# The product with V as split fp32r products over 128 stationary columns, in a two-layer hybrid attention block

## The chip, the core and the metric

The kernel runs on one core of a Trainium2 chip. The metric is the device time of one execution in microseconds; the time before is the median of three runs. A core has TensorE (PE in the profile; PEld is its weight load), VectorE (DVE), ScalarE (ACT), GpSimd (POOL) and SyncE (SP), which here issues the DMAs. The engines run side by side, each its own instructions in order.

## The reference

Two layers over 1024 latent tokens and 256 context tokens of width 1024. Each layer mixes tokens with three head groups and then applies an MLP. What matters here is the softmax and its product with V, once for each group:

```python
# A: 4 heads, 2 KV heads, windowed (|i-j| <= 128) plus all context keys, with a sink logit
p = softmax(concat([s_loc, s_ctx, sink_logit]))
out = einsum(p[..., :n_loc], vb) + einsum(p[..., n_loc:n_loc + n_ctx], v_ctx)
# B: 4 heads, 2 KV heads, all 1280 keys, RMS-normalised q and k
p = softmax(einsum(qg, k) * dh ** -0.5);  out = einsum(p, v)
# C: 8 heads, low-rank q and kv, shared rotary key of 32
s = einsum(q_nope, k_nope) + einsum(q_rope, k_rope)
p = softmax(s * 96 ** -0.5);              out = einsum(p, v)
```

Head size of V is 64 everywhere. Context queries (layer 0 only) see the context keys alone. The output projection, the residuals, the normalisations and the squared-ReLU MLP of width 4096 are outside the change. All is fp32.

## The kernel before

Tokens are cut into 10 tiles of 128: tiles 0 and 1 are context, 2 to 9 latent. Large products are made of fp32r products of high and low parts: a value x is split into a high part of type fp32r (a copy) and the low part x - high (a subtraction), and three products (high-high, high-low, low-high) stand for one.

A layer runs in stages. The input projection (`Proj`) makes queries, keys and V of A and B for each token tile, and the 416 columns that C starts from, all kept in SBUF. Then comes attention: A and B heads alternately, then the eight C heads, each in windows of one head and its query groups (two groups of four latent tiles; in layer 0 also the group of the two context tiles). The output projection and the MLP follow.

One step of attention (`step`) is one head and one query tile: PE writes the scores of up to 1280 keys into PSUM, DVE takes the maximum (L798, L1012), ScalarE the exponential with the sum (L771), DVE the sum of two partial sums where there are two (C heads, L783) and the reciprocal (L784), and the row is scaled by it. `NORM` says which engine scales: GpSimd for A (L789), DVE for B and C (L791).

The product with V (`Attn.products`, L819) goes over the key tiles of a unit, that is one head and one query group. For each key tile PE transposes the four tiles of P into one of two PSUM banks (`tr`, L827); ScalarE copies the bank to SBUF (`ptS`, L832, three places), which frees the bank; PE multiplies (L842). The product is in fp32: the stationary operand is V, 64 columns, the moving one 256 query columns, and the two halves of the queries go to the two halves of the array's columns (`tile_position`), 2 x 2 matmul records in the profile. The sums of a unit grow in one PSUM bank (`pvb`); DVE copies it to SBUF (`ys`, L866), and two DMAs bring it to memory.

C's preparation (`AttnC`) transposes the low-rank columns, and makes V of all eight heads (`prep_v`, L1230) ahead of the first C head; for each head it makes keys (`prep_k`) and queries (`prep_q`). Where a split has room it leaves its PSUM bank first: ScalarE copies to SBUF, DVE casts the high part (L710 for keys, L1304 for queries), GpSimd subtracts (L713, L1307). The queries' rotary part is turned by DVE and GpSimd (L1293, L1297, L1301).

The order of all this is not written by hand. Each operation is given to `Plan` with its engine, a rough time, what it needs and a key; `Plan.run` plays the operations through on a model of the engines and emits them in the order of their starts. At run time each engine keeps to that order. GpSimd cannot pass an instruction that waits, nor can DVE or ScalarE.

## Time and profile before

| | us |
|---|---|
| median of three runs | 3544.21 (3541.7 to 3546.61) |
| span of the profiled execution | 3540.4 |
| the span's busy time: PE / DVE / ACT / POOL | 3398.3 / 2011.7 / 1290.8 / 856.1 |
| scores of A and B: first start to last end, layer 0; layer 1 | 228.9 to 463.9; 2120.0 to 2328.9 |
| last product with V, layer 0; layer 1 | 869.0; 2715.4 |

The median lies 3.8 us above the profiled span. A row that groups instructions gives line, engine, operation, output and inputs by the program's names, partitions x elements, count; behind the bar busy time and the mean of one in ns, then the engine's idle time ahead of them and what ended it. The busy time of matmuls counts overlapping ones once; their own ends are modelled, so rows of the timeline are read from start to start.

### The profile page before, as it was taken

Reading aid. Unit: us, or ns where it says so; the run is one execution under the profiler, and the core shown is the slowest. Engines: PE = TensorE matmul, PEld = TensorE weight load, DVE = VectorE, ACT = ScalarE, POOL = GpSimd, SP = SyncE. Lnnn points to the kernel's source line nnn. Section 1 sums busy time; section 2 is a strip of 40 time slices with the busy share of each in tenths; the row PEclk is TensorE's granted clock in tenths of the full one; section 3 lists DMA queues with packets and bytes.
Section 4 is the critical chain, followed back from the end, with each engine's and each line's share of the span. In section 5 each row is a group of like instructions: output and inputs, shape, how many; then the busy total and the mean of one; then the engine's idle time right before and its main releaser. Section 6 shows DMA issues by size and latency. Waiting matters only on the chain. (4 is left out here: it accounts for less than half of the span.)

```text
span 3540.4 us, 46962 instructions
## 1 busy us (share of the span) xinstructions
PE 3398.3 (96%) x18628; PEld 2577.9 (73%) x18628; DVE 2011.7 (57%) x3640; ACT 1290.8 (36%) x2568; POOL 856.1 (24%) x690
## 2 busy tenths in 40 slices
PE   7999999999899999999997999999998899999998
PEld 4776666665778787888885886666665778888887
DVE  3466777775763333333437656766676854444446
ACT  2136666665322121212121226666665222222222
POOL 1243332220421010111015433332223611111113
PEclk9999999999999999999998999999999999999999
DMA  7500100004213332201113200000014011111121
GB/s 259 161 8 11 29 8 8 9 28 129 85 66 102 96 95 90 90 30 48 36 36 126 90 1 8 28 8 7 7 50 141 24 42 48 48 48 48 51 87 48
DMA packets 155677, 206.99 MB, mean 58 GB/s; under 512 B 9808, under 2 KB 107584, under 8 KB 154432
## 3 DMA queue, kind: packets, MB, share of 16 engines
q1 hardware_dynamic: 152576, 192.12, 17.1%
q10 hardware_dynamic: 2736, 11.80, 0.8%
q8 instruction: 146, 2.39, 0.3%
q14 instruction: 75, 0.61, 0.1%
q0 software_dynamic: 144, 0.07, 0.0%
HBM read 179.86 MB, written 24.15 MB: 58 GB/s over the span
## 5 line engine op out<-in xcount | busy, mean ns | idle before, releaser
L1794 DVE TENSOR_TENSOR acc<-acc,o 128x512 f32<-128x512 f32 x518 | 332.6, 683 | 406.6 <-PE o L1783 406.5
L106 POOL TENSOR_TENSOR al<-r,ah 128x512 fp32r<-128x512 f32 x136 | 159.8, 1175 | 1184.0 <-ACT ah L105 1099.4
L832 ACT COPY ptS<-tr 128x512 f32<-128x512 f32 (+2 forms) x624 | 336.5, 552 | 273.9 <-PE tr L827 268.9
L1783 PE MATMUL o<-w2h,ah 128*128 128x512 f32 x1080 | 342.9, 398 | 11.0 <-ACT ah L105 7.7
L1783 PE MATMUL o<-w2h,al 128*128 128x512 f32 x1080 | 334.9, 391 | 0.7 <-DVE al L106 0.6
L1783 PE MATMUL o<-w2l,ah 128*128 128x512 f32 x1080 | 335.4, 392 | 0.0
L1675 DVE TENSOR_TENSOR r<-r 128x512 f32<-128x512 f32 x150 | 102.4, 682 | 368.3 <-ACT r L1674 368.3
L1661 PE MATMUL tr<-hTl,w1h 128*128 128x512 f32 (+1 forms) x856 | 307.3, 359 | 4.4 <-DVE hTl L1579 4.4
L827 PE MATMUL tr<-ident,PB 128*128 128x128 f32 x1920 | 303.6, 283 | 4.9 <-DVE PB L791 3.7
L1661 PE MATMUL tr<-hTh,w1h 128*128 128x512 f32 (+1 forms) x856 | 307.1, 359 | 0.0
L1661 PE MATMUL tr<-hTh,w1l 128*128 128x512 f32 (+1 forms) x856 | 306.8, 358 | 0.0
L827 PEld LDWEIGHTS tr<-ident,PB 128*128 128x128 f32 x1920 | 211.4, 141 | 130.9 <-issue 109.0
L1327 PE MATMUL c<-kb,cq 96*128 96x512 f32 (+1 forms) x1200 | 288.3, 371 | 4.3 <-ACT PC L771 2.5
L798 DVE TENSOR_REDUCE nx<-c 128x1 f32<-128x256 f32 (+1 forms) x272 | 214.2, 793 | 103.4 <-PE c L1327 96.2
L105 ACT CAST w2h<-w2s 128x1024 fp32r<-128x1024 f32 x58 | 60.9, 1050 | 539.6 <-DVE w2s L1653 332.3
L1327 PEld LDWEIGHTS c<-kb,cq 96*128 96x128 f32 x1200 | 196.9, 188 | 76.1 <-issue 18.4
L1783 PEld LDWEIGHTS o<-w2h,ah 128*128 128x128 f32 x1080 | 197.9, 189 | 60.1 <-ACT ah L105 8.8
L1783 PEld LDWEIGHTS o<-w2h,al 128*128 128x128 f32 x1080 | 203.2, 188 | 46.0 <-DVE al L106 2.1
L1783 PEld LDWEIGHTS o<-w2l,ah 128*128 128x128 f32 x1080 | 203.6, 189 | 44.3
L842 PE MATMUL pvb<-ptS,vc 128*64 128x256 f32 x1344 | 215.5, 401 | 10.8 <-ACT ptS L832 8.9
L771 ACT ACTIVATE PB<-c,nx 128x256 f32<-128x256 f32 (+1 forms) x256 | 202.4, 798 | 28.2 <-DVE nx L748 27.4
L1503 PE MATMUL o<-wo,hTh 128*128 128x512 f32 x576 | 184.1, 401 | 0.0
(485 smaller groups left out, 6602.9 us busy)
## 6 DMA issues: line engine op xcount, KB each, us to landing
mw<-in_w_mod SPq DMA_DIRECT2D x80, 512.0 KB
w1s<-in_w_fc SPq DMA_DIRECT2D x62, 512.0 KB
w2s<-in_w_fc SPq DMA_DIRECT2D x62, 512.0 KB
yf<-ydr SPq DMA_DIRECT2D x18, 512.0 KB
wst<-in_w_in SPq DMA_DIRECT2D x16, 512.0 KB
ydr<-ys SPq DMA_DIRECT2D x128, 64.0 KB
wos<-in_w_out SPq DMA_DIRECT2D x16, 512.0 KB
x1dr<-xt SPq DMA_DIRECT2D x10, 512.0 KB
```

Source lines behind the costliest of these rows:

```text
L106: (el or V.tensor_tensor)(out=lo, in0=src, in1=f32(hi), op=OP.subtract)
L771: S.activation(out=st["P"][:, o:o + w], in_=f(), func=AF.Exp, scale=scale, bias=st["nx"][:, 0:1], accum_out=st["sm"][:, i:i + 1])
L798: V.tensor_reduce(out=st["nx"][:, i:i + 1], in_=view, axis=AX.X, op=OP.max, negate=True)
L827: PE.transpose(ptp[:, j * 128:(j + 1) * 128], u["P"][j][:, pc(j):pc(j) + 128], ident)
L832: S.copy(out=st["t"][:, c0:c1], in_=ptp[:, c0:c1])
L842: PE.matmul(pvb[64 * half:64 * half + 64, c0 - b:c1 - b], lhsT=u["V"](tt), rhs=st["t"][:, c0:c1], start=(idx == 0), stop=(idx == len(kts) ...
L1327: PE.matmul(p, lhsT=a[:, qs], rhs=b[:, c0:c1], start=(n == 0), stop=(n == 2), skip_group_check=True)
L1503: PE.matmul(p, lhsT=self.place(t, a, k // 4)[:, k % 4, :], rhs=self.wo[n, k][b], start=(k == 0 and first), stop=(k == 7 and last))
L1661: PE.matmul(p[:, 0:w], lhsT=a[:, k, :], rhs=o.hT[i][b, k // 4][:, k % 4, :], start=(k == 0 and first), stop=(k == 7 and last))
L1675: V.tensor_tensor(out=r[:, 0:w], in0=r[:, 0:w], in1=r[:, 0:w], op=OP.mult)
L1783: PE.matmul(p[i], lhsT=a[:, ts_], rhs=b[:, i * 512:(i + 1) * 512], start=(first and n == 0), stop=(last and n == 2))
L1794: V.tensor_tensor(out=o, in0=o, in1=p[i], op=OP.add)
```

## The change

The product with V becomes one of split parts. V is stored as 128 stationary columns, 64 of its high part and beside them 64 of its low part, both fp32r. P is split when it leaves the transposes' bank: ScalarE copies the high part as before, now cast to fp32r, and DVE subtracts to get the low part, after which the bank is free. PE multiplies the 128 columns with the high and then with the low part of P, 512 query columns each, in the whole array. Rows 0 to 63 of the bank `pvb` then hold the part from V's high columns, rows 64 to 127 that from the low ones: ScalarE copies the lower rows out, DVE adds the upper ones, and one DMA stores the result.

```diff
-    PTS = 3
+    PTS = 2
-    NORM = {k: [dict(p='POOL', d='DVE')[x] for x in v] for k, v in zip('ABC', 'pppp dddd dddd'.split())}
+    NORM = {k: [dict(p='POOL', d='DVE')[x] for x in v] for k, v in zip('ABC', 'pppp pppp pppp'.split())}
...
             def copied(ptp, st, js):
-                st["t"] = M([128, 512], F32, "ptS", bufs=PTS)
-                S.copy(out=st["t"][:, c0:c1], in_=ptp[:, c0:c1])
+                both = M([128, 2, 512], F32R, "ptS", bufs=PTS)
+                st["t"] = both[:, 0, cols(js)], both[:, 1, cols(js)]
+                S.copy(out=st["t"][0], in_=ptp[:, cols(js)])
+
+            def rest(ptp, st, js):
+                V.tensor_tensor(out=st["t"][1], in0=ptp[:, cols(js)], in1=f32(st["t"][0]), op=OP.subtract)
 
             def product(st, idx):
-                for half in range(2):
-                    PE.matmul(pvb[64 * half:64 * half + 64, c0 - b:c1 - b], lhsT=u["V"](tt), rhs=st["t"][:, c0:c1],
-                              start=(idx == 0), stop=(idx == len(kts) - 1), tile_position=(0, 64 * half),
-                              skip_group_check=True)
+                for n, part in enumerate(st["t"]):
+                    PE.matmul(pvb[:, cols(js)], lhsT=u["V"](tt), rhs=part, start=(idx == n == 0),
+                              stop=(n == 1 and idx == len(kts) - 1), skip_group_check=True)
...
-                cp = plan.add("ACT", t_act(128 * len(js)), lambda tr=tr, st=st, js=js: copied(tr.slot, st, js), [tr], k + KCOPY, "pt", [tr])
+                hi = plan.add("ACT", t_act(128 * len(js)), lambda tr=tr, st=st, js=js: copied(tr.slot, st, js), [tr], k + KCOPY, "pt")
+                lo = plan.add("DVE", t_dve(128 * len(js)), lambda tr=tr, st=st, js=js: rest(tr.slot, st, js), [hi], k + KCOPY, None, [tr])
...
-                V.tensor_copy(st["y"][:, 0:w], pvb[:, 0:w])
+                S.copy(out=st["y"], in_=pvb[64:128, 0:w])
+                V.tensor_tensor(out=st["y"], in0=pvb[0:64, 0:w], in1=st["y"], op=OP.add)
```

All softmax scaling now is GpSimd's: the 192 rows of 1280 and 24 of 256 that DVE scaled join the 72 that GpSimd had. V takes twice the room, so other things are cut smaller or leave SBUF: C's 416 columns go to memory after the projection (`cdr`) and come back in pieces ahead of C (`load_kv`, `load_cq`, eleven loads in all); V of C is made for four heads at a time (`prep_v(half, i)`), the second four while heads 3 and 4 run; the weights of C's queries come in two halves; B's and C's keys lie in tiles of up to 512 tokens, and the projected rows of A and B in two tiles of 512 columns. In the input projection V of A and B is split for each token tile by four small copies on ScalarE and four subtractions on DVE. The finished sums have one place instead of two.

PE's order in the layer 1 C sweep, in a run of rounds without scores between (`tr` are the two banks, `PB` the rows of P, `vc` C's V). Before:

```order
L842 MATMUL pvb<-ptS_15277,vc_451_17077 64x256 x2
L827 MATMUL tr_64<-ident_66,PB_416_15402 128x128
L827 MATMUL tr_64<-ident_66,PB_418_15442 128x128
L827 MATMUL tr_64<-ident_66,PB_419_15494 128x128
L827 MATMUL tr_64<-ident_66,PB_421_15544 128x128
L842 MATMUL pvb<-ptS_15291,vc_452_17117 64x256 x2
```

And now:

```order
L881 MATMUL pvb<-ptS_15950,vc_496_17870 128x512 x2
L865 MATMUL tr_63<-ident_66,PB_420_15861 128x128
L865 MATMUL tr_63<-ident_66,PB_428_15901 128x128
L865 MATMUL tr_63<-ident_66,PB_434_15932 128x128
L865 MATMUL tr_63<-ident_66,PB_442_15989 128x128
L881 MATMUL pvb<-ptS_15959,vc_496_17870 128x512 x2
```

The alternation stays; the two narrow products of a key tile became two wide ones.

DVE's order in the same sweep, from a cast of keys (`kb`) on (`nx` are maxima, `sm` sums, `c` scores). Before:

```order
L710 CAST kb_439_16664<-sp_409_15353 64x512
L798 TENSOR_REDUCE nx_15251<-c_449_0_16989 128x1
L783 TENSOR_TENSOR sm_15239<-sm_15239 128x1
L784 RECIPROCAL sm_15239<-sm_15239 128x1
L798 TENSOR_REDUCE nx_15251<-c_449_1_16990 128x1
L791 TENSOR_SCALAR PB_392_15236<-PB_392_15236,sm_15239 128x1280
L748 TENSOR_SCALAR nx_15251<-nx_15251 128x1
L710 CAST kb_439_16664<-sp_423_15760 64x512
```

And now:

```order
L748 CAST kb_479_17476<-sp_449_16061 64x512
L909 TENSOR_TENSOR ys_16049<-pvb,ys_16049 64x512
L876 TENSOR_TENSOR ptS_15959<-tr_63,ptS_15959 128x512
L837 TENSOR_REDUCE nx_15918<-c_492_0_17794 128x1
L822 TENSOR_TENSOR sm_15904<-sm_15904 128x1
L823 RECIPROCAL sm_15904<-sm_15904 128x1
L837 TENSOR_REDUCE nx_15918<-c_492_1_17795 128x1
L876 TENSOR_TENSOR ptS_15950<-tr_64,ptS_15950 128x512
L787 TENSOR_SCALAR nx_15918<-nx_15918 128x1
L748 CAST kb_482_17579<-sp_457_16471 64x512
```

The scaling (L791) is gone from the piece, and the subtractions (L876) and the addition of finished sums (L909) stand in it.

GpSimd's order there. Before, only the work on keys and queries:

```order
L713 TENSOR_TENSOR kb_439_16664<-sp_409_15353,kb_439_16664 64x512
L713 TENSOR_TENSOR kb_439_16664<-sp_423_15760,kb_439_16664 64x512
L1297 TENSOR_TENSOR qf_16856<-qf_16856,trig_16244 32x512
L1307 TENSOR_TENSOR cq_16841<-qf_16856,cq_16841 96x512
L713 TENSOR_TENSOR kb_439_16664<-sp_389_15229,kb_439_16664 64x256
```

And now:

```order
L828 TENSOR_TENSOR PB_420_15861<-PB_420_15861,sm_15988 128x1280
L751 TENSOR_TENSOR kb_488_17697<-sp_449_16061,kb_488_17697 64x512
L828 TENSOR_TENSOR PB_428_15901<-PB_428_15901,sm_16005 128x1280
L751 TENSOR_TENSOR kb_489_17708<-sp_457_16471,kb_489_17708 64x512
L828 TENSOR_TENSOR PB_434_15932<-PB_434_15932,sm_16043 128x1280
L1359 TENSOR_TENSOR qf_17667<-qf_17667,trig_16978 32x512
L828 TENSOR_TENSOR PB_442_15989<-PB_442_15989,sm_16065 128x1280
L1369 TENSOR_TENSOR cq_17654<-qf_17667,cq_17654 96x512
```

A scaling (L828) now stands ahead of nearly every piece of that work.

## Rows read from the trace of the kernel before

**Rows 1.** Part 1 of the page: busy time, share, instructions.

```profile
PE 3398.3 (96%) x18628; PEld 2577.9 (73%) x18628; DVE 2011.7 (57%) x3640; ACT 1290.8 (36%) x2568; POOL 856.1 (24%) x690
```

**Rows 2.** Four attention stretches: length, then PE, PEld, DVE, ACT, POOL busy (instructions), clock, DMA.

```profile
229.00:470.00 241.00, 230.11 (x1505) 154.01 (x1504) 173.65 (x407) 159.50 (x349) 98.61 (x90) 0.99 0.06 17
470.00:869.00 399.00, 390.07 (x2384) 255.30 (x2382) 286.19 (x582) 249.25 (x559) 81.59 (x63) 1.00 0.11 33
2120.00:2340.00 220.00, 210.65 (x1378) 137.00 (x1377) 155.57 (x322) 146.13 (x298) 81.17 (x67) 1.00 0.06 16
2340.00:2715.00 375.00, 364.26 (x2154) 233.82 (x2154) 258.23 (x495) 230.53 (x496) 89.59 (x59) 0.98 0.11 35
sum 1235.00, PE 1195.09 PEld 780.13 DVE 873.64 ACT 785.42 POOL 350.95; mean PE 298.77 PEld 195.03 DVE 218.41 ACT 196.35 POOL 87.74
```

**Rows 3.** The same view: one C head of layer 0, one of layer 1.

```profile
592.10:637.70 45.60, 45.09 (x279) 29.78 (x278) 34.09 (x70) 28.29 (x64) 10.11 (x8) 1.00 0.03 8
2438.60:2481.20 42.60, 42.45 (x256) 27.52 (x255) 29.38 (x59) 26.29 (x58) 9.30 (x7) 1.00 0.03 7
```

**Rows 4.** Timeline of PE, layer 0 C sweep: start, us, line, operation, count.

```profile
621.86 0.65 PE L842 MATMUL pvb<-ptS,vc 128*64 128x256 f32 x4
622.44 0.66 PE L827 MATMUL tr<-ident,PB 128*128 128x128 f32 x4
623.03 0.65 PE L842 MATMUL pvb<-ptS,vc 128*64 128x256 f32 x4
```

**Rows 5.** Timeline of PE, layer 1 C sweep.

```profile
2440.44 0.66 PE L827 MATMUL tr<-ident,PB 128*128 128x128 f32 x4
2440.86 1.63 PE L1327 MATMUL c<-kb,cq 96*128 96x512 f32 x6
...
2450.77 1.66 PE L1327 MATMUL c<-kb,cq 96*128 96x512 f32 x6
2452.27 0.60 PE L827 MATMUL tr<-ident,PB 128*128 128x128 f32 x4
2452.62 0.36 PE L1257 MATMUL tr<-kvh,uk 128*64 128x256 f32 x1
```

**Rows 6.** Busy time in 50 us of the layer 1 MLP.

```profile
3000.00:3050.00 50.00, 50.00 (x222) 41.43 (x221) 23.24 (x31) 8.88 (x12) 5.17 (x4) 1.00 0.14 43
```

**Rows 7.** Stretches of rows 2, by tile, sums alone: ptS, PB, PC, ys.

```profile
sum 1235.00, PE 389.44 PEld 126.11 ACT 336.50; mean PE 97.36 PEld 31.53 ACT 84.13
sum 1235.00, PE 303.61 PEld 211.42 DVE 182.18 ACT 307.60; mean PE 75.90 PEld 52.85 DVE 45.54 ACT 76.90
sum 1235.00, PE 9.95 PEld 5.28 DVE 9.02 ACT 13.77; mean PE 2.49 PEld 1.32 DVE 2.26 ACT 3.44
sum 1235.00, DVE 30.82; mean DVE 7.71
```

**Rows 8.** Groups of instructions by line and shape, whole span.

```profile
L1794 DVE TENSOR_TENSOR acc<-acc,o 128x512 f32<-128x512 f32 x518 | 332.6, 683 | 406.6 <-PE o L1783 406.5
L832 ACT COPY ptS<-tr 128x512 f32<-128x512 f32 x512 | 294.7, 587 | 232.7 <-PE tr L827 228.2 <-DVE PB L791 0.6
```

**Rows 9.** The same view: GpSimd scaling head group A.

```profile
L789 POOL TENSOR_TENSOR PA<-PA,sm 128x640 f32<-128x640 f32 x48 | 60.7, 1265 | 165.8 <-DVE sm L784 151.7 <-PE pvb L842 8.8 <-DVE nx L748 5.1
L789 POOL TENSOR_TENSOR PA<-PA,sm 128x512 f32<-128x512 f32 x16 | 17.4, 1090 | 38.8 <-DVE sm L784 38.5
```

**Rows 10.** A layer 1 head; timeline, layer 0; line L783 with ns min/median/max.

```profile
L710 DVE CAST kb<-sp 64x512 fp32r<-64x512 f32 x2 | 0.8, 417 | 0.9 <-ACT sp L706 0.9
...
612.64 1.72 POOL L1297 TENSOR_TENSOR qf<-qf,trig 32x512 f32<-32x512 f32 x1 [13.20 <-ACT qf L1287]
613.25 1.26 DVE L710 CAST cq<-sp 96x256 fp32r<-96x256 f32 x1
614.65 0.74 POOL L713 TENSOR_TENSOR cq<-sp,cq 96x256 fp32r<-96x256 f32 x1 [0.29 <-DVE cq L710]
...
L783 DVE TENSOR_TENSOR sm<-sm x128: 147/150/2299, 483.3 to 2688.0; 128x1 f32<-128x1 f32 x128
```

More of the change, by code (lines that the diff above doesn't have):

```diff
@@ L100, in hybrid_dit_kernel @@
     ydr = [dram.tile([1024, T], F32, name=f"ydr{l}") for l in range(DEPTH)]
+    cdr = [dram.tile([T, 416], F32, name=f"cdr{l}") for l in range(DEPTH)]
     x1dr = dram.tile([T, D], F32, name="x1dr")
@@ L1247, in prep_v @@
[L1247 removed]
+                uvh, uvl = self.uv
+                for n in range(2):
+                    kvh, kvl = (self.kv(s, (2 * i + n) * 128, (2 * i + n) * 128 + 128) for s in range(2))
+                    p = pt[:, n * 256:n * 256 + 256]
+                    PE.matmul(p, lhsT=kvh, rhs=uvh[:, hs], start=True, stop=False)
+                    PE.matmul(p, lhsT=kvh, rhs=uvl[:, hs], start=False, stop=False)
+                    PE.matmul(p, lhsT=kvl, rhs=uvh[:, hs], start=False, stop=True)
@@ new lines, in parts, with hi, lo @@
+            def parts(pt):
+                v = self.vc[half, i]
+                return v[:, :, :, 0:64], v[:, :, :, 64:128], pt.rearrange("p (t h d) -> p t h d", t=2, d=64)
+            def hi(pt):
+                self.vc[half, i] = M([128, 2, 4, 128], F32R, f"vc{i}")
+                h, _, src = parts(pt)
+                S.copy(out=h, in_=src)
+            def lo(pt):
+                h, lo, src = parts(pt)
+                V.tensor_tensor(out=lo, in0=src, in1=f32(h), op=OP.subtract)
+            return [("PE", 0.72, product), ("ACT", t_act(512), hi), ("DVE", t_dve(512), lo)]
@@ L1376, in plan @@
                 at.gate(cq[2][0], base, EC - 8)
-            two = [plan.add("DVE", 0.75, lambda i=i: self.second_keys(i), kr, base - 4) for i in range(2)]
-            two[1].after.append(two[0])
-            for t in range(NT):
-                ops = chain(self.prep_v(t), base - 3 + t // 2, kv + uv)
-                at.gate(ops[0], base, EC)
-                vs[t] = ops[-1]
+            two = [plan.add("DVE", 0.75, lambda i=i: self.second_keys(i), kr, base - 4) for i in range(3)]
+            late = base + 4 * sum(len(g) for g in groups)
+            values = {(half, i): chain(self.prep_v(half, i), (late - 2 if half else base - 3) + i, kv + uv)
+                      for half in range(2) for i in range(NT // 2)}
             units, products, cross, ends_q, keys = [], [], [], [], {}
@@ L1396, in plan @@
                 units += us
+            for (half, i), ops in values.items():
+                if half == 0:
+                    at.gate(ops[0], base, EC)
+                    continue
+                for u in units:
+                    if u["h"] == 3:
+                        ops[0].after += [u["pv"][tt] for tt in (2 * i, 2 * i + 1) if tt in u["pv"]]
             all_scores = lambda v: [o for sc in v["score"].values() for o in sc]
@@ L1453, in gates @@
             l = self.l
-            self.gate = {v: bcast(f"gate{v}", gdr[l][v, 0]) for v in range(2 if l == 0 else 1)}
+            n = 2 if l == 0 else 1
+            both = M([128, n, D], F32, "gates")
+            self.gate = {v: both[:, v, :] for v in range(n)}
+            for v in range(n):
+                ld(out=self.gate[v], in_=gdr[l][v, 0].partition_broadcast(128))
         def norm_before(self):
```

250 lines of the change are left out of this document (140 added, 110 removed).

## The prediction

> **What bounds the kernel now.** I read the page first: TensorE (PE) is busy for 96% of the span [rows 1]. A busy PE alone says little, so I cut out the stretches that the change touches. The four windows of [rows 2] are layer 0's sweep of the A and B heads (229 to 470 us), its C heads with the tail (470 to 869), and the same two of layer 1. Together they last 1235 us. In them PE is busy 1195 us, 97%; VectorE (DVE) 874, ScalarE 785, GpSimd (POOL) 351. The other 2305 us are projections and MLP. There the change adds small DVE and ScalarE copies for V and a round trip of the C columns through memory, all beside PE work; I cost them at nothing, and at 10 us if the first loads back come late.
>
> Inside the C sweep the work repeats: a head of layer 0 takes 45.6 us, one of layer 1 42.6, and PE is busy for all but 0.5 and 0.15 us of it, while DVE works 34.1 and 29.4 us [rows 3]. So PE's own stream is the bound, and DVE has a quarter to a third of its time free. The question is what the change takes from the first and puts on the second.
>
> **The change, part 1: the product with V on PE.** Start to start, a product with V (both halves of the queries, one key tile) holds PE for 0.58 us (621.86 to 622.44), and four transposes between two such products 0.59 (to 623.03) [rows 4]: 1.17 us a key tile. Where scores follow the transposes these take 0.42 (2440.44 to 2440.86), a round of 1.00. Between two full-width fp32r products they take 0.35 (2452.27 to 2452.62), and the six score products ahead of them 1.50 [rows 5]. In the MLP an fp32r product of 512 columns takes 50/222 = 0.225 us [rows 6]. So the six stream for 1.35 us and a change of kind costs 0.15. The new product is two fp32r products of 512 columns in the whole array, 0.45 us; with transposes of 0.35 and one change of kind a round is 0.95. That saves 0.05 to 0.22 a key tile; runs of rounds are common, so I take 0.2 for each of the 624, 125 us, with 31 and 137 as ends. PE's need falls from 1195 to about 1070 us.
>
> **Part 2: what DVE gets.** From the tiles ptS, PB, PC and ys over the four windows, in turn [rows 7]:
> - added: a subtraction for each of the 624 copies out of the transposes' bank (the low part of P). It has the copy's shape. The copies take ScalarE 336.5 us at 587 ns for 512 columns; a DVE operation with one input in PSUM and one in SBUF takes 683 ns for 512 [rows 8]. So 336.5 x 683/587 = 391.5 us.
> - removed: the softmax scaling of B and C, 182.2 (PB) and 9.0 (PC), which goes to POOL, and the copies of the finished sums, 30.8.
> - added: 64 additions of 512 columns and 16 of 256 for the finished sums, 64 x 0.683 + 16 x 0.4 = 50.1; ten more evacuations of V, 6.8.
>
> The sum is 873.6 + 391.5 - 182.2 - 9.0 - 30.8 + 50.1 + 6.8 = 1100 us. DVE's need has passed PE's. ScalarE gains some 40 us (80 copies of finished sums at half a microsecond) on 785 and stays below both.
>
> **Part 3: what the scaling does on POOL, and to DVE.** POOL scales head group A already: 1265 ns for 640 columns, 1090 for 512 [rows 9]. For 1280 columns that gives 2.1 us by the slope and 2.5 by proportion; I take 2.3. With 192 of these and 24 small ones, POOL goes from 351 to about 800 us of 1235, two thirds busy, no bound by itself. But DVE and POOL do not run freely beside each other. A DVE cast of 512 columns takes 417 ns alone; in the layer 0 sweep a cast of 256 columns that began at 613.25, while POOL's multiplication ran from 612.64 to 614.36, ended at 614.51, after 1.26 us. The sum of two [128x1] columns ahead of each reciprocal has a median of 150 ns and a maximum of 2299 [rows 10]. These DVE operations read and write SBUF alone; they seem to wait for the end of POOL's running instruction. The subtraction, which reads PSUM, is not of them: its like in the MLP shows 683 ns in the mean of 518 [rows 8].
>
> Each C head has 17 such operations (8 sums, 3 casts of keys, 2 each of the rotation's two steps and of the casts of queries), 272 in all. Along DVE's new order in a layer 1 head I set each against the scaling that the reciprocal before it releases: the first two casts of keys stand 0.6 and 1.3 us behind one and wait 1.7 and 1.0; the rotation's first step waits 1.2, twice; its second 0.5, twice; three of the sums 0.2 to 0.8 behind POOL's own key and query work; the rest nothing. That is 7 to 8 us a head, of which some 1.8 are in today's durations: 6 us more, 96 over 16 heads. Behind a waiting one stand subtractions, for which PE's next product waits, and reductions, which free PE's score banks. For some sixty casts in the A and B stretches I take 0.6 us each, 36. Together 132 us. Bounds: nothing, if all fall between POOL's instructions; and 332 x 1.15 = 380 us, if each meets half a scaling.
>
> The Trainium skill, GPSIMD Engine Reference, section 3.1, measures 4497 ns for a GpSimd addition of 2048 fp32 columns, which makes an estimate of 2.8 us for 1280; [rows 9] are below it. By that figure the waits would be a fifth longer and the time some 28 us more.
>
> **Part 4: longer hold of three PSUM banks.** The transposes' two banks were free after ScalarE's copy, now after DVE's subtraction. In a run of rounds with no scores between, PE does a product (0.45), transposes (0.35) and then waits for copy (0.59), subtraction (0.68) and three hand-overs of 0.14 each (614.51 to 614.65 in [rows 10]) to the second product after: 2.5 us for two rounds, 1.25 a round, where part 1 had 0.95 and today's is 1.17. In seven such rounds a head this costs 0.08 x 7 x 16 = 9 us against today, more if a reduction stands ahead on DVE. The bank of the finished sums is now held through a ScalarE copy and a DVE addition (0.59 + 0.68) instead of one DVE copy of 0.4: 0.9 us and a hand-over more for 80 units, beside transposes and scores that PE can do meanwhile. In the sum both are the share of time in which the bounding engine idles.
>
> **The sum.** DVE needs 1100 + 132 = 1232 us of stages that last 1235. Today's bound, PE, is idle for 3% of them; I give DVE the same 3%: 1232/0.97 = 1270, 35 us more than now. The profiled execution's span of 3540.4 becomes 3575. The median of the runs, 3544.2, is 3.8 above the span, so 3579, rounded to 3580.
>
> **Rivals.**
> 1. *The dearer products go and DVE keeps up: faster.* The waits for POOL are inferred from few collisions, while POOL is a quarter busy; DVE's stream could settle so that they fall into POOL's idle time, since each scaling starts from DVE's own reciprocal. With no waits the stages take 1100/0.97 = 1134 us, 101 less: 3443. With half of them (66) 1202: 3511. For it: PE's saving is sure where products with V and transposes alternate, and 1100 is below 1235. Against: DVE must never be short of work. I take 3495. The Trainium skill, TensorEngine Tiling, Key Properties, says that a change of tiling mode drains TensorE; by that the 0.13 us by which a product with V exceeds 0.45 belong to its column tiles and go with them, with which [rows 4, 5] agree.
> 2. *Hand-overs decide: clearly slower.* If DVE in its fixed order idles 8% instead of 3%, because each subtraction waits for PE and ScalarE with only two banks in turn, the stages take 1232/0.92 = 1339 us: 3648. It decides once a round costs more than today's 1.17 us though no engine is full.
> 3. *Nothing comes of it.* PE saves its part, DVE's waits and the hand-overs take it back to within 7 us: 3544. That is a narrow target between the others.
>
> **How the numbers follow.** Slower by DVE's fullness and POOL's scalings, 3580: 0.45. Hand-overs on top, about 3648: 0.17. Faster, about 3495: 0.30. Same: 0.08. A measurement of this kernel tells about 0.2%, 7 us, from no change. The low end takes the waits at a fifth of my value, (1100 + 27)/0.97 = 1162, that is 3471, so 3470; the high end the 8% case with some 10 us for the loads back, 3660. Slower 0.62, same 0.08, faster 0.30. As the cases have both signs, the likeliest one's own range is 3555 to 3625.
>
> **What would show it.** In the new trace, start to start: a product with V of 0.45 us and transposes of 0.35 (part 1). DVE at 95% or more in the four stages and PE below 90% (part 2); if both stay below 90%, rival 2 holds. The sums of two columns with a mean well over 0.2 us, casts of keys of a microsecond or more that end just behind a POOL instruction (part 3); if they stay short and layer 1's C heads take under 40 us, rival 1 holds. PE's waits for DVE's subtraction ahead of products with V (part 4). Everything outside the four stages within 10 us of now. I am wrong altogether if the scalings on POOL take much more than 2.5 us, or if PE stays over 96% busy.

## The result: 154 us slower, and the profile after

The changed kernel takes 3699.0 us (median of four runs, 3697.0 to 3702.9) against 3544.7: a ratio of 1.0439, with a 95% interval of 1.0424 to 1.0454. I had forecast slower, at 3580 with a range up to 3660. The way was right; I had 36 us of the 154 that came, and the range ended 39 us too low.

The span of the profiled execution grew by 157.3 us, to 3697.7. I cut both traces at the first scores of heads A and B and at the last product with V of each layer:

| us | before | after | difference |
|---|---|---|---|
| up to layer 0's first scores | 228.9 | 246.5 | +17.6 |
| layer 0's attention | 640.1 | 714.8 | +74.7 |
| between | 1251.0 | 1254.1 | +3.1 |
| layer 1's attention | 595.4 | 657.7 | +62.3 |
| the rest | 825.0 | 824.5 | -0.5 |

So 137 us lie in the attention ("the stretches" below: the two rows on attention together, 1235.5 us before and 1372.5 after), 17.6 ahead of it, nothing to speak of elsewhere. Part 1 of the page of the kernel after, to be read against [rows 1]:

```profile
PE 3366.4 (91%) x17536; PEld 2718.4 (74%) x17536; DVE 2298.2 (62%) x4158; ACT 1347.1 (36%) x2712; POOL 1320.1 (36%) x976
```

Its stretches by windows, columns as in [rows 2]:

```profile
246.50:961.30 714.80, 603.09 (x3333) 477.52 (x3333) 598.48 (x1213) 437.28 (x964) 414.40 (x275) 0.95 0.10 28
2215.40:2873.10 657.70, 559.17 (x3032) 441.31 (x3031) 557.84 (x1033) 401.04 (x835) 391.80 (x222) 0.95 0.10 28
sum 1372.50, PE 1162.26 PEld 918.83 DVE 1156.32 ACT 838.31 POOL 806.20; mean PE 581.13 PEld 459.41 DVE 578.16 ACT 419.16 POOL 403.10
```

The same for instructions on the tile `ptS` alone, as in [rows 7], where DVE had none before:

```profile
sum 1372.60, PE 453.55 PEld 216.63 DVE 390.57 ACT 339.40; mean PE 113.39 PEld 54.16 DVE 97.64 ACT 84.85
```

The reader is to see that no engine is full any more. Before, PE was busy for 97% of the stretches; now PE for 85%, at a mean clock of 0.95, and DVE for 84%. PE's longest waits over the whole span (engine, tile and line, what ended the wait: us in total, times, longest):

```profile
PE pvb L881 <- DVE ptS L876: 97.0, 96, 2.8
PE ab L1004 <- ACT PB L810: 22.4, 35, 2.0
```

One such wait, in layer 1's C sweep (timeline: start, us, engine, line, operation, idle time before it):

```profile
2531.17 1.28 DVE L1363 TENSOR_TENSOR qf<-qf,r 32x512 f32<-32x512 f32 x1
...
2531.78 0.58 ACT L873 CAST ptS<-tr 128x512 fp32r<-128x512 f32 x1 [1.94 <-PE tr L865]
...
2532.41 0.50 PE L881 MATMUL pvb<-ptS,vc 128*128 128x512 f32 x1
2532.48 0.29 DVE L748 CAST kb<-sp 64x256 fp32r<-64x256 f32 x1
2532.62 0.58 ACT L873 CAST ptS<-tr 128x512 fp32r<-128x512 f32 x1 [0.26 <-PE tr L865]
2532.69 0.41 DVE L1366 CAST cq<-qf 96x512 fp32r<-96x512 f32 x1
2533.03 1.54 DVE L837 TENSOR_REDUCE nx<-c 128x1 f32<-128x256 f32 x2
...
2534.49 1.27 DVE L876 TENSOR_TENSOR ptS<-tr,ptS 128x512 fp32r<-128x512 f32 x2
...
2535.22 0.59 PE L881 MATMUL pvb<-ptS,vc 128*128 128x512 f32 x1 [2.31 <-DVE ptS L876]
```

PE issues the product with the high part at 2532.41 and needs the low part for the second. ScalarE's copy of that round ended at 2532.36; DVE comes to the subtraction at 2534.49, after a rotation, two casts and two reductions. Meanwhile nothing can go ahead on PE: the next transposes stand behind the product. PE stands still for 2.31 us. Then its clock falls (three pieces of 3.5 us around that place, columns as above, the granted clock behind POOL's count):

```profile
2531.90:2535.40 3.50, 1.19 (x8) 0.72 (x6) 3.47 (x7) 1.04 (x2) 1.95 (x3) 1.00 0.00 0
2535.40:2538.90 3.50, 3.50 (x13) 2.90 (x14) 1.18 (x3) 1.08 (x3) 0.00 (x0) 0.51 0.00 0
2538.90:2542.40 3.50, 3.50 (x22) 2.80 (x21) 2.81 (x8) 3.45 (x9) 1.28 (x1) 1.00 0.00 0
```

After a piece in which PE works 1.19 of 3.5 us, the granted clock is 0.51, its lower level of 1.2 GHz, and 13 matmuls start where 22 do in the next piece (they are not all of one size). In the stretches the clock falls 29 times and is low for 137 us; before, 3 times and 21 us (counted in the trace's record of the granted clock). Whether that costs time is a question for an experiment.

The 17.6 us ahead of the attention have a cause of their own. The timeline of SyncE's queue of DMAs:

```profile
50.30 0.43 SPq L2098 DMA_DIRECT2D xin<-in_x  x1
69.45 0.33 SPq L498 DMA_DIRECT2D cdr<-pjc  x1
69.83 0.33 SPq L247 DMA_DIRECT2D lnrows<-in_ln_g  x1
```

And PE's longest wait of the first 247 us:

```profile
PE pvb L249 <- DMA lnrows<-in_ln_b: 11.3, 1, 11.3
```

SyncE issues nothing from 50.7 to 69.45: the first store of C's columns waits for the first token tile, and the loads of the layer norm's rows stand behind it. PE waits 11.3 us for them.

### The profile page after: what moved, and what is told of

Same layout as the page of the kernel before. It is cut to its first block, busy times and chain, and to the rows that moved or that the text cites. A ratio compares the mean times of both kernels' runs of the same rounds, so it can differ in the third digit from the quotient of the medians.

```text
span 3697.7 us, 46075 instructions
## 1 busy us (share of the span) xinstructions
PE 3366.4 (91%) x17536; PEld 2718.4 (74%) x17536; DVE 2298.2 (62%) x4158; ACT 1347.1 (36%) x2712; POOL 1320.1 (36%) x976
## 3 DMA queue, kind: packets, MB, share of 16 engines
q1 hardware_dynamic: 154640, 200.11, 17.6%
## 5 line engine op out<-in xcount | busy, mean ns | idle before, releaser
L828 POOL TENSOR_TENSOR PB<-PB,sm 128x1280 f32<-128x1280 f32 x192 | 451.3, 2351 | 383.6 <-DVE sm L823 197.5
L873 ACT CAST ptS<-tr 128x512 fp32r<-128x512 f32 (+2 forms) x624 | 339.4, 551 | 288.6 <-PE tr L865 263.4
L876 DVE TENSOR_TENSOR ptS<-tr,ptS 128x512 fp32r<-128x512 f32 (+2 forms) x624 | 390.6, 638 | 67.8 <-ACT ptS L873 63.3
L881 PE MATMUL pvb<-ptS,vc 128*128 128x512 f32 x672 | 253.8, 448 | 77.2 <-DVE ptS L876 65.1
L865 PEld LDWEIGHTS tr<-ident,PB 128*128 128x128 f32 x1920 | 246.6, 147 | 81.2 <-DVE ptS L876 12.6
L881 PE MATMUL pvb<-ptS,pjv 128*128 128x512 f32 (+3 forms) x576 | 199.7, 415 | 43.2 <-DVE ptS L876 31.9
L1389 PEld LDWEIGHTS c<-kb,cq 96*128 96x128 f32 x1200 | 205.3, 193 | 45.3 <-ACT PB L810 14.0
```

What stands on the lines that cost most here:

```text
L828: G.tensor_tensor(out=keys, in0=keys, in1=sm[:, 0:1].to_broadcast([128, n - sinks]), op=OP.mult)
L865: PE.transpose(ptp[:, j * 128:(j + 1) * 128], u["P"][j][:, pc(j):pc(j) + 128], ident)
L873: S.copy(out=st["t"][0], in_=ptp[:, cols(js)])
L876: V.tensor_tensor(out=st["t"][1], in0=ptp[:, cols(js)], in1=f32(st["t"][0]), op=OP.subtract)
L881: PE.matmul(pvb[:, cols(js)], lhsT=u["V"](tt), rhs=part, start=(idx == n == 0), stop=(n == 1 and idx == len(kts) - 1), skip_group_check=True)
L1389: PE.matmul(p, lhsT=a[:, qs], rhs=k(b, c0, c1), start=(n == 0), stop=(n == 2), skip_group_check=True)
```

## The experiments

All are the changed kernel with an edit, but for one that is the kernel before. The time of the kernel before, on the same chips, was between 3542.8 and 3544.5 in every group. Stretches and busy time are read as above. e1, e7, e9 and e10 leave all or most of the low part of P out of the result. The edits of e1 to e4, e7, e8, e10 and e11 leave DVE's order as it was; e5, e6, e9 and e12 to e18 are planned anew, so each of them differs from the others by its order too.

| run | median us | stretches us | DVE / PE busy there |
|---|---|---|---|
| before | 3544.7 | 1235.5 | 874 / 1196 |
| after | 3699.0 | 1372.5 | 1156 / 1162 |
| e7_no_low_norm_dve | 3524.1 | 1200.1 | 882 / 1092 |
| e1_no_low | 3549.4 | 1223.6 | 849 / 1100 |
| e10_short_sub | 3634.8 | 1306.7 | 961 / 1131 |
| e2_norm_dve | 3712.1 | 1385.7 | 1205 / 1175 |
| e3_before_pool | 3586.8 | 1277.2 | 831 / 1216 |
| e11_fill | 3692.7 | 1370.2 | 1154 / 1248 |
| e6_casts_act | 3664.0 | 1338.2 | 1057 / 1151 |
| e12_combo | 3623.8 | 1313.6 | 1045 / 1160 |
| e13_first_4 | 3661.1 | 1349.8 | 1068 / 1168 |

**Is it the subtractions, or the scaling on GpSimd?** e1 leaves out the subtractions and keeps the order of everything else.

```diff
-                for n, part in enumerate(st["t"]):
+                for n, part in enumerate([st["t"][0]] * 2):
...
-                V.tensor_tensor(out=st["t"][1], in0=ptp[:, cols(js)], in1=f32(st["t"][0]), op=OP.subtract)
+                pass
```

> The changed kernel without the 624 subtractions: both products with V read the high part of P, so the low part is left out of the result; every other instruction keeps its place. PE has the same matmuls, DVE 391 us less. Theory A (the subtraction comes late because it stands behind other work in DVE's queue, PE stands still for it and its clock falls): the four attention stretches, 1373 us now, come down to what PE needs, about 1070 to 1130, fewer than ten falls of the clock in them; time 3400 to 3460. Theory B (the softmax scaling on GpSimd, 2.35 us each and in the way of DVE, is what holds the rounds up): scalings and collisions are all still there, so the time stays above 3600.

Measured: 3549.4 us. With the subtractions go 150 us, so theory B is out as the main cause. But A's number is missed too: PE's work is that of the changed kernel, and still the stretches last 1223.6 us and not 1070 to 1130. e1's stretches (the windows' sum), and the two longest of PE's waits over its span, which are for the exponentials to free the banks of the scores:

```profile
sum 1223.60, PE 1099.71 PEld 896.58 DVE 848.86 ACT 835.69 POOL 807.62; mean PE 549.86 PEld 448.29 DVE 424.43 ACT 417.85 POOL 403.81
```

```profile
PE ab L1004 <- ACT PB L810: 25.6, 35, 2.0
PE c L1389 <- ACT PB L810: 19.1, 31, 2.8
```

e7 takes the scaling of B and C off GpSimd as well, by the edit of e2 below.

> The changed kernel without the subtractions (both products read the high part of P, the low part is left out of the result) and with the scaling of B and C on DVE as before: what is left of the change is the two wide products. Against the run without subtractions it is the scaling on GpSimd alone that goes. If the scaling on GpSimd ate PE's saving there: 3460 to 3510, about what the wide products save by themselves. If the wide products save nothing: 3540 to 3560.

Measured: 3524.1, between the two expectations. PE's busy time in the stretches falls from 1196 to 1092 us, as I had it from the rounds, but the stretches get shorter by 35 only. The rest has become idle time: PE is idle for 108 us, where it was for 40. e7's stretches, and three of PE's waits over its span, which in the kernel before were 10.7, 2.4 and 0.8 us:

```profile
sum 1200.10, PE 1091.75 PEld 888.96 DVE 882.45 ACT 832.84 POOL 349.50; mean PE 545.88 PEld 444.48 DVE 441.23 ACT 416.42 POOL 174.75
```

```profile
PE ab L1004 <- ACT PB L810: 20.7, 32, 2.0
PE pvb L881 <- DVE ys L909: 16.2, 23, 1.9
PE c L1389 <- ACT PB L810: 13.2, 37, 1.2
```

PE now waits for the exponentials, which free the banks of the scores, and for the finished sums, which leave their bank by two engines and one place where it was one engine and two places. e7 also has all else that the change brought (two places for the copies, smaller tiles of keys, the columns' round trip), so 35 us is the worth of the wide products together with these. To see whether an order made for another DVE was to blame, e9 told the planner of the missing subtractions.

```diff
-    WST = 2
+    WST = 1
...
-                lo = plan.add("DVE", t_dve(128 * len(js)), lambda tr=tr, st=st, js=js: rest(tr.slot, st, js), [hi], k + KCOPY, None, [tr])
-                after = [lo] + ([self.last_pv] if self.last_pv else []) + (self.last_ys if idx == 0 else [])
+                after = [hi] + ([self.last_pv] if self.last_pv else []) + (self.last_ys if idx == 0 else [])
```

> The changed kernel without the subtractions (the high part of P is multiplied twice, the low part is left out of the result), with the planner told so: it puts every instruction in a new order for a DVE that has 391 us less; the scaling stays on GpSimd. One staging buffer of the MLP's weights goes for room, so only the four stretches are compared: 1224 us in the old order. If the old order is what kept PE idle there: 1110 to 1170. If GpSimd's scalings and the depth of the buffers set it: 1200 to 1230.

Measured: 1209.2 us in the stretches (3561.8 in all, with 33 us more between them for the missing buffer). The new order gives 14 us against e1, not a hundred. So the wide products with what came along are worth 35 us here, some 50 if those 14 come on top, and not what PE saves.

**What of a subtraction costs: its length or the link?**

```diff
-                V.tensor_tensor(out=st["t"][1], in0=ptp[:, cols(js)], in1=f32(st["t"][0]), op=OP.subtract)
+                n = 64 if len(js) == 4 else 128 * len(js)
+                V.tensor_tensor(out=st["t"][1][:, 0:n], in0=ptp[:, cols(js)][:, 0:n], in1=f32(st["t"][0])[:, 0:n], op=OP.subtract)
+                if len(js) == 4:
+                    st["t"] = st["t"][0], st["both"][:, 64:576]
```

> The changed kernel with the 512 full-width subtractions cut to their first 64 columns, so that most of the low part of P is left out of the result (the second product reads those 64 columns and 448 of the high part). All hand-overs stay: transposes, copy, subtraction, product; only DVE's time for one goes from 0.68 to some 0.13 us, 283 us in all. Theory L (DVE's queue is too long, and the subtraction comes late by the work ahead of it): as without subtractions, 3550 to 3590. Theory H (the extra link in the chain is what costs, whatever its length): 3630 to 3690.

Measured: 3634.8, theory H's number. The short subtraction takes 218 ns and not 130, so the subtractions are 238 us shorter, and the time fell by 64; the other 85 us of e1 are still there. e10's group of short subtractions (count | busy, mean ns | idle before), the sum of its stretches, and PE's longest wait:

```profile
L878 DVE TENSOR_TENSOR ptS<-tr,ptS 128x64 fp32r<-128x64 f32 x512 | 108.7, 218 | 103.1 <-ACT ptS L874 99.9
```

```profile
sum 1306.70, PE 1131.32 PEld 909.74 DVE 961.50 ACT 835.66 POOL 806.97; mean PE 565.66 PEld 454.87 DVE 480.75 ACT 417.83 POOL 403.48
```

```profile
PE pvb L885 <- DVE ptS L878: 68.6, 54, 2.8
```

DVE is busy for 74% of the stretches here, about as much as before the change (71%), and PE still waits 68.6 us for it. The runs so far make a ladder for the stretches: 1235.5 before; 1200.1 with the wide products and the rest of the change; 1223.6 with the scaling on GpSimd; 1306.7 with a short subtraction in each round; 1372.5 with the whole one. The steps are -35, +24, +83, +66. DVE's busy time rises by 113 us in the third step and by 195 in the last, so for each us of its work the short link is the dearer one (0.73 us against 0.34).

What the link meets can be read from the traces: the start of each subtraction less the end of the copy that it follows, summed over the 624, is 346 us in the changed kernel and still 319 in e10, half a microsecond a round. So the short subtraction, too, stands behind DVE's other work in the fixed order; theory H's number came, but the place in the queue that theory L named is a part of what the link costs, and e10 does not part the two.

**The scaling, both ways.** e2 issues B's and C's scaling on DVE, in the changed kernel; e3 on GpSimd, in the kernel before.

(`sinks` is set for head group A alone.)

```diff
-                if e == "POOL":
+                if e == "POOL" and sinks:
```

```diff
-                if e == "POOL":
+                if True:
```

> The changed kernel with the scaling of B and C issued on DVE again, at the place in the order where GpSimd's stands. DVE gets 191 us back and loses the 63 us by which its casts and rotations were longer beside GpSimd: 1156 - 63 + 191 = 1284 us of work in stretches of 1373. Theory A: DVE is fuller and the subtractions later, 3720 to 3850. Theory B: the collisions and the long scalings go, 3560 to 3660.

> The kernel before with the scaling of B and C issued on GpSimd at the place where DVE's stood: this part of the change alone. DVE loses 191 us and gets back up to 63 from collisions. Theory A: PE stays the bound, within 15 us of the time before (3530 to 3560). Theory B: transposes wait for scalings of 2.35 us in place of 0.95, and DVE for GpSimd; slower by 40 us or more.

Measured: e2 3712.1, slower by 13, just short of A's bounds; e3 3586.8, slower by 43 than the kernel before, as B had it and A had not. With subtractions, a fuller DVE is the worse; without them, GpSimd's scaling is. Its price shows on DVE. In e3 a scaling of 191 us left DVE, and DVE's busy time fell by 43 only (874 to 831): what stayed became about 148 us longer (131 added up instruction by instruction, since busy time counts overlaps once). The groups for the two steps of the rotation on DVE, in the kernel before and in e3:

```profile
L1293 DVE TENSOR_TENSOR r<-qf,trig 32x512 f32<-32x512 f32 x32 | 30.6, 956 | 12.4 <-ACT qf L1287 11.9
L1301 DVE TENSOR_TENSOR qf<-qf,r 32x512 f32<-32x512 f32 x32 | 24.6, 768 | 1.0
...
L1293 DVE TENSOR_TENSOR r<-qf,trig 32x512 f32<-32x512 f32 x32 | 61.2, 1912 | 25.3 <-ACT qf L1287 25.0
L1301 DVE TENSOR_TENSOR qf<-qf,r 32x512 f32<-32x512 f32 x32 | 40.7, 1273 | 1.0
```

In the changed kernel's order the same shows. e2's groups for the casts of keys and the sums of two columns, with DVE scaling:

```profile
L748 DVE CAST kb<-sp 64x512 fp32r<-64x512 f32 (+3 forms) x54 | 23.5, 436 | 1.2 <-ACT sp L744 0.5
L822 DVE TENSOR_TENSOR sm<-sm 128x1 f32<-128x1 f32 x128 | 21.7, 169 | 11.5 <-ACT PB L810 11.0
```

And the changed kernel's, with the scaling itself:

```profile
L828 POOL TENSOR_TENSOR PB<-PB,sm 128x1280 f32<-128x1280 f32 x192 | 451.3, 2351 | 383.6 <-DVE sm L823 197.5
...
L748 DVE CAST kb<-sp 64x512 fp32r<-64x512 f32 (+3 forms) x54 | 52.2, 967 | 1.8 <-ACT sp L744 1.2
L822 DVE TENSOR_TENSOR sm<-sm 128x1 f32<-128x1 f32 x128 | 32.6, 254 | 8.7 <-ACT PB L810 8.3
```

A cast of keys takes 436 ns in the mean where DVE scales, 967 where GpSimd does. The subtraction, which reads PSUM, takes 683 ns for 512 columns in the one and 682 in the other. In the changed kernel's trace each of the 24 casts of keys longer than 0.7 us ends 147 to 282 ns after the end of a GpSimd instruction that ran beside it, and each of the 27 sums longer than 0.25 us 13 to 24 ns after one: they wait for its end, as the prediction had supposed. The Trainium skill, SBUF — State Buffer, "SBUF: two separate sides", has one port pair that GpSimd shares with DVE's operations on two SBUF inputs and its fast modes, and that the first to come holds for its whole instruction. These rows agree with it.

**Does the slow clock cost time?** e11 fills PE's stands. In the 68 rounds in which PE stood for 0.9 us or longer between the two products with V, it adds products of a zero block.

```diff
+                    for _ in range(0 if n else FILL.get(rounds[0], 0)):
+                        b = js[0] * 128
+                        PE.matmul(pvb[0:64, b:b + 256], lhsT=ident[0:64, 64:128], rhs=f32(part)[0:64, 0:256], start=False,
+                                  stop=False, skip_group_check=True)
```

> The changed kernel with 239 added products that add zero, at some 0.43 us each, in the 68 rounds in which PE stood still for 0.9 to 3.1 us (124 us in all) between its two products with V: PE works there instead of standing still, and waits for the subtraction no longer than before. If PE's clock falls follow these stands and cost time (137 us of the stretches at half clock, 21 before; 58 us at most): falls in the stretches go from 29 to under 15, 3640 to 3685. If PE's slow clock is beside the path, or the falls stay: 3695 to 3720.

Measured: 3692.7, between the two expectations, 6 us less and within the spread of the runs (3689.7 to 3702.7, against 3697.0 to 3702.9). The fill did much of what it should: PE's wait for the subtraction fell from 97.0 to 10.5 us, the falls from 29 to 15, the time at low clock from 137 to 82. e11's wait over its span, and its stretches:

```profile
PE pvb L883 <- DVE ptS L878: 10.5, 37, 1.0
```

```profile
sum 1370.20, PE 1247.51 PEld 959.45 DVE 1154.16 ACT 836.48 POOL 806.58; mean PE 623.75 PEld 479.72 DVE 577.08 ACT 418.24 POOL 403.29
```

PE is busy for 85 us more, and the stretches are as long as they were. So the falls of the clock, though the most visible thing in the trace, follow the waits, and 55 us less at the lower level, half the speed, could save 27 us at most; 6 came, or nothing. That the round is waiting for DVE anyway while PE works slowly is my reading of it. (Where a fill ran longer than the wait it may have cost something itself, so a few us more than 6 could be the clock's; the 82 us that are left were not tried.)

**The store in SyncE's queue.** e4 issued the layer norm's loads ahead of the store (`ln_turn` is what is left of `ln_rows`); e8 issues each store one token tile later.

```diff
         pr = startup(W)
+        ln_rows()
...
-                    bg.append(ln_rows)
+                    bg.append(ln_turn)
```

> The changed kernel with the eight loads of the layer norm's rows issued ahead of the first tile's projection, so that they no longer stand on SP behind the first store of C's columns. Theory C (the store waits for the first tile's columns and the loads wait behind it; PE stands still 11.3 us before their transpose, then runs 10.2 us at half clock): that wait goes, 12 to 17 us less, 3682 to 3687. Rival D (those 11 us only put off a wait that comes anyway, for weights or a split): less than 4 us.

```diff
-                ld(out=cdr[self.l][t * 128:(t + 1) * 128, c0:416], in_=pc[:, c0:416])
+                self.kept.append(lambda: ld(out=cdr[self.l][t * 128:(t + 1) * 128, c0:416], in_=pc[:, c0:416]))
+                while len(self.kept) > (0 if len(self.pj) >= NT else 1):
+                    self.kept.pop(0)()
```

> The changed kernel with each store of C's columns issued one token tile later on SP, so that no load stands behind a store whose data are not there. The projection ahead of the first scores of layer 0 lasts 17.6 us longer than before. Theory C (loads wait behind the first store): that goes, 3682 to 3688. Rival: the 17.6 us come from the added split of V and the clock; 3695 to 3703.

e4 measured 3701.6: no gain, for the loads that stand next in the queue, of modulation weights, are now the late ones (e4's longest wait of PE in the first 243 us):

```profile
PE pvb L127 <- DMA mw<-in_w_mod: 9.3, 1, 9.3
```

e8 measured 3689.4, 10 us less; the first scores start at 232.9 instead of 246.5, which leaves 4 of the 17.6 us without a cause. The culprit is the store, not the loads that happened to stand behind it.

**What helps, and what doesn't.** e5 plans the two products of a key tile apart; e6 gives DVE's casts of keys and queries to ScalarE; e12 is e5, e6 and e8 together.

```diff
-            stages.append(("DVE", 0.13 + 0.00052 * n, lambda x, k=k, hi=hi: V.tensor_copy(hi(), src(st["t"], k))))
+            stages.append(("ACT", t_act(n), lambda x, k=k, hi=hi: S.copy(out=hi(), in_=src(st["t"], k))))
...
-                pv = plan.add("PE", 2 * (128 * len(js) + 32) / 2400, lambda st=st, idx=idx: product(st, idx), after, k + KPV, None, [hi])
+                ph = plan.add("PE", (128 * len(js) + 32) / 2400, lambda st=st, idx=idx: product(st, idx, 0), after, k + KPV)
+                pv = plan.add("PE", (128 * len(js) + 32) / 2400, lambda st=st, idx=idx: product(st, idx, 1),
+                              [lo, ph] + ([self.last_pv] if self.last_pv else []), k + KPV, None, [hi])
```

> The changed kernel with the two products of a key tile planned apart: the one with the high part of P may go as soon as ScalarE's copy is there, with transposes or scores between it and the one with the low part. Same work on every engine. Theory A (PE stands still behind the subtraction in its own fixed order): part of its 97 us of such waits and of the clock falls behind them go, 3620 to 3680. Rival: the transposes' two banks are free no earlier, so PE only waits at another place; 3690 to 3710.

> The changed kernel with the casts of keys and queries that DVE made from SBUF given to ScalarE: DVE 114 us less (52.2 + 24.2 + 21.7 + 15.7), of which 45 us are lengthening beside GpSimd, ScalarE some 85 more on 838 of 1373. If DVE's queue is what delays the subtraction: 3620 to 3670. Rival: ScalarE's copies, which the subtraction follows, become the late ones; 3690 to 3730.

> The changed kernel with the products planned apart, the casts on ScalarE, and the stores of C's columns one tile later, all together. Singly they took 5, 35 and 10 us. If they add up: 3640 to 3660. If the casts' 35 us and the products' 5 are the same waits: 3655 to 3670. None of it reaches the time before.

Measured: 3694.6, 3664.0 and 3623.8. Alone, the split is worth 4 us, hardly clear of the spread, as its rival had it; with 99 us off DVE, time falls by 35; together they take 75, more than the 49 of the parts and beyond either expectation. Why is open; each of the three has an order of its own. PE's wait for the subtraction is halved; 21.5 us are now for ScalarE's copy. e12's longest waits of PE, and one of ScalarE for the maxima:

```profile
PE pvb L883 <- DVE ptS L879: 47.9, 70, 2.5
PE ab L1010 <- ACT PB L813: 23.6, 35, 2.6
PE pvb L883 <- ACT ptS L876: 21.5, 37, 3.1
```

```profile
ACT PB L813 <- DVE nx L790: 68.6, 75, 2.3
```

From e12, e13 and e14 let the subtraction go ahead of other work on DVE, e15 gives every second scaling back to DVE, and e18 plans with the trace's prices; e17 is e6 with a third place for the copies.

```diff
-                        t, o = min(((t, o) for t, o in starts if t <= first + PATIENCE), key=lambda x: (x[1].key, x[1].n))
+                        t, o = min(((t, o) for t, o in starts if t <= first + (AHEAD if o.ahead else PATIENCE)), key=lambda x: (x[1].key, x[1].n))
```

`AHEAD` is 0.4 us in e13 and 0.8 in e14.

> The run with all three together (products planned apart, casts on ScalarE, stores later; 3624), and the planner lets a subtraction go first on DVE where it is ready within 0.4 us of whatever else could start. Same work. In the changed kernel the subtractions start 346 us in all behind the copies that they follow, 137 of it under reductions for the maxima; in the run of three together 228 and 73. If that place behind the reductions is what is left of the cost: delay under 190, time 3590 to 3615. If the reductions, now later themselves, hold back the exponentials and the scores as much: 3615 to 3640.

> The same with 0.8 us in place of 0.4. If the subtraction's place is what costs, more goes than with 0.4: 3575 to 3610. If the reductions' delay costs as much: 3620 to 3660.

Measured: 3661.1 and 3713.3, slower than e12 by 37 and 89, beyond either expectation. The delay of the subtractions (start of each less the end of the copy that it follows, summed over the 624) did fall, from 228 to 148 us in e13, but no further in e14 (146). What grew is another wait: DVE comes to the subtraction before ScalarE's copy is there and stands idle, since it keeps to its order. e12, e13 and e14:

```profile
DVE ptS L879 <- ACT ptS L876: 76.5, 142, 3.3
DVE ptS L880 <- ACT ptS L877: 106.9, 240, 2.1
DVE ptS L880 <- ACT ptS L877: 177.1, 286, 4.1
```

The maxima come later as well. The same waits as above in e13:

```profile
PE pvb L884 <- DVE ptS L880: 35.9, 68, 3.9
PE ab L1012 <- ACT PB L814: 34.6, 44, 2.7
PE pvb L884 <- ACT ptS L877: 28.5, 44, 2.2
```

```profile
ACT PB L814 <- DVE nx L791: 88.2, 82, 4.3
```

PE's wait for the subtraction falls by 12 us; its waits for banks of scores and for copies rise by 18, and the exponentials' wait for the maxima from 68.6 to 88.2. These waits of PE come to 6 us more; its idle time in the stretches grows by 29, so they are only part of it.

```diff
-    NORM = {k: [dict(p='POOL', d='DVE')[x] for x in v] for k, v in zip('ABC', 'pppp pppp pppp'.split())}
+    NORM = {k: [dict(p='POOL', d='DVE')[x] for x in v] for k, v in zip('ABC', 'pppp pdpd pdpd'.split())}
```

> The run with all three together, and every second scaling of B and C on DVE again (0.95 us each, about 96 more), GpSimd's share halved. With the whole scaling on DVE the changed kernel took 13 us more, and without subtractions 24 us less, so the sign should turn with DVE's load, which here is 1045 us of 1314. If GpSimd's long scalings cost more than 91 us of DVE: 3600 to 3620. If DVE's queue costs more: 3630 to 3660.

```diff
-    PTS = 2
+    PTS = 3
```

> The run with the casts on ScalarE (3664), and three places in place of two for the copied P with its low part, as the kernel before had for its copies: the copy of a third round need not wait for a product. If two places hold the rounds back: 3610 to 3645. If only the transposes' two banks do, and DVE's turn: 3655 to 3672.

```diff
-        return 0.04 + 0.00086 * n
+        return 0.04 + 0.00107 * n
...
-        return 0.09 + 0.001 * n
+        return 0.08 + 0.00118 * n
```

> The run with all three together (3624), with the planner's prices for ScalarE and DVE raised to what the trace shows (0.59 us for a copy of 512 columns, 0.68 for a subtraction, 1.21 for a reduction of 1024): it plans with the engines as full as they are. If the order, made with prices 9 to 17 per cent too low, is what costs: 3570 to 3605. If not: 3610 to 3640.

Measured: e15 3673.8 (50 slower than e12: DVE has 58 us more), e17 3664.0 (no change from e6), e18 3674.5 (51 slower); e15 and e18 lie beyond both of their ranges. e18 has e12's work in another order, so an order alone can be worth 51 us, and the differences between e12 and e13 to e15 cannot be put down to their edits with certainty. Neither a third place for copies nor truer prices in the planner helped, and no run that computes the whole product beats the kernel before.

## Why the prediction missed

**Part 1, PE's saving: right in size, wrong in worth.** Where [rows 4] had 0.58 and 0.59, a product with V takes 0.47 us (2420.01 to 2420.48) and four transposes 0.35 (to 2420.83), in e7's layer 1 C sweep:

```profile
2420.01 0.63 PE L881 MATMUL pvb<-ptS,vc 128*128 128x512 f32 x2
2420.48 0.60 PE L865 MATMUL tr<-ident,PB 128*128 128x128 f32 x4
2420.83 0.71 PE L881 MATMUL pvb<-ptS,vc 128*128 128x512 f32 x2
```

PE's busy time fell by 104 us, within 31 to 137 and near the 125 taken. These rows are the best case: in alternation a round takes 0.82 to 1.00 us in that sweep, around the 0.95 forecast. But its worth was taken for granted: in the sum it only handed the bound to DVE, and rival 1 counted on stretches of 1134 to 1202 us with 1100 to 1166 us of work on DVE. e7 has 882 us there and needs 1200: PE's idle time grows from 40 to 108 us as soon as it is no longer full, and 35 us are left. The wait for the bank of the finished sums, which part 4 put beside PE's other work at no cost, is part of that (16.2 us in e7 and 12.3 in the changed kernel, 2.4 before).

**Part 2, DVE's work: right.** The subtractions take 390.6 us (391.5 forecast), the additions of finished sums 49.0 (50.1). Without waits for GpSimd, DVE's work comes to 1098 us (1100).

**Part 3, GpSimd: the mechanism right, its size in the sum too large by a third or more.** A scaling takes 2351 ns (2.3 us), and GpSimd is busy for 806 us (800). DVE's busy time lies 58 us above those 1098 (1156), where I had 132. But busy time counts overlapping instructions once: added up one by one, the operations that were there before are about 90 us longer. Against the same order with the scaling on DVE (e2), they are 114 us longer one by one, 138 in busy time, and in e3 131 and 148; part of it stood in the kernel before already, in the durations that I started from.

**Part 4 and the sum: the step that failed.** I costed the link between copy and product at 9 us and some hand-overs, and let DVE idle for 3% since PE, the bound before, idled for 3%. DVE idles for 16% (1156 of 1372.5). By e10 the link with a short operation (218 ns) costs 83 us, the rest of the operation's length 66 more. With the work that DVE really got, my formula would have given 1156/0.97 = 1192 us, 44 less than before, and a faster kernel: two errors of opposite sign, of which the one in the waits hid part of the one in the idle share. That the way came out right is in part luck. Rival 2 was the right mechanism, with 8% where it should have had 16; the high end of the range was made of that 8%. Rival 1 fell on the same number: with waits at the half that I gave it, the kernel still is slower.

Why 3% held for PE and not for DVE is argued from the waits and not shown by a run of its own: before, PE had a product or transposes ready nearly always, since DVE and ScalarE worked ahead of it. Now DVE stands in two loops, that of a row (scores, maximum, exponential, sum, scaling) and that of a round (transposes, copy, subtraction, product), and has one fixed order for both. In e13 and e14, where the subtraction goes first, DVE waits longer for the copy and the maxima come later; that no order could serve both loops is not shown. How much a third bank for the transposes would give is open; it was not tried, since score tiles take the rest of that memory here.

**The round trip of C's columns: wrong place.** I allowed 10 us for loads back that come late. No engine shows a wait for a load back; the store held up others on SyncE's queue, for 10 us (e8).

**What I had asked the trace.** Products of 0.45 and transposes of 0.35: yes. In the changed kernel's own trace 0.46 and 0.35 (from 2563.05) where nothing holds PE up, 0.55 for a product elsewhere (from 2574.49). DVE at 95%, PE below 90%: DVE 84, PE 85, which the prediction named as the mark of rival 2. Sums of two columns well over 0.2 us: 254 ns, but their mean was 206 before (the 150 that I had was the median), so the mark told little. Casts of a microsecond that end just behind a GpSimd instruction: 967 ns in the mean, where it was 624, and the ends are as told with e2's rows: yes. Nothing outside the stretches over 10 us: no, 17.6 ahead of them.

## What to carry over

When a change takes work from the full engine and gives it to one that is seven tenths busy but stands between the others, do not add up busy time and carry the old idle share along: ask how many loops pass through that engine, and price each new link (here 83 us for 624 links with an operation of 0.2 us in each, some 0.13 us a link, and 66 more for the whole operation). A saving on the bound is worth only as much as the distance to the next chain of waits, which a run with the cost left out shows at once. And a slow clock beside long waits may be a symptom: fill PE's idle gaps before counting it as a cost.

## What the runs showed that I had not expected

- Filling PE's stands brought its time at the lower clock from 137 to 82 us, and the time went down by 6 us of 3699, within the spread of the runs.
- A DVE subtraction from PSUM takes 218 ns for 64 columns and 683 for 512: shortening it to an eighth leaves a third of it.
- With scalings on GpSimd in the kernel before, DVE's first rotation step went from 956 to 1912 ns in the mean; two thirds to three quarters of the 191 us that left DVE came back in this way (131 us instruction by instruction, 148 in busy time).
- Letting the subtractions go first on DVE made it stand idle for ScalarE's copies, 76.5, 106.9 and 177.1 us in e12, e13 and e14.
- One store that waits at the head of SyncE's queue kept it from issuing anything for 18.7 us (50.73 to 69.45), and moving the loads behind it only changed which load was late.
